# Row sums of the two widest diagonal pieces on GpSimd, and the running sum's matmuls at the block's end

## Chip, cores and metric

The kernel runs on one core of a Trainium2 chip. The metric is the device time of one execution in microseconds (us). Three executions of the kernel before took 2401.36, 2403.96 and 2404.28 us; the median, 2403.96 us, is the time before.

## What is computed

One decoder layer over 16 meta tokens and 2048 tokens of width 1024: a layer norm, one wide input projection, two token mixers side by side (attention with a forget gate, and a causal pooling), each gated, one output projection, and a last layer norm. The change touches the attention alone, 16 heads of 64 channels:

```python
s = jnp.einsum('bqhd,bkhd->bhqk', q_blk, k).astype(jnp.float32) * scale
s = s + jnp.transpose(c_blk, (0, 2, 1))[..., :, None] - c_k[:, :, None, :]
mask = key_pos[None, :] <= q_pos[:, None]
s = jnp.where(mask[None, None], s, -jnp.inf)
p = jax.nn.softmax(s, axis=-1).astype(v.dtype)
return jnp.einsum('bhqk,bkhd->bqhd', p, v)
```

The softmax needs the sum over all keys of the exponentials, for every query. That row sum is what the change moves about.

## The kernel before

**Stages.** Up to about 1350 us the kernel normalizes, projects and pools. Then comes the attention, until about 2225 us, with the output projection of the pooling half mixed into it; the rest of the output projection and the last layer norm follow.

**Blocks and units.** The attention works through 64 blocks, one for a head h and a group j of 512 queries (`seqn`, L763: j = 0 to 3 of one head after the other; the last two heads are interleaved). A block is a list of units (`units`, L903). A unit is one PSUM bank of up to 512 columns: 4j + 1 units with one tile of 128 keys against all 512 queries (the last of these, number 4j, lies on the diagonal and is masked in part), one unit 4j + 1 with the 400 queries from column 112 on, and a last unit 4j + 2 with three short pieces of 272, 144 and 16 columns. So a block has 4j + 3 units: 3, 7, 11 or 15.

**What a unit does.** `emit_s` (L959): two matmuls make the scores `s` in PSUM (four banks), a third adds the mask on the diagonal. ScalarE writes the exponential as `ph` in TensorE's rounded format, and once more in full precision over `s`. `emit_pl` (L996): VectorE subtracts `ph` from that, which is the rest `pl`; it also frees the bank of `s`. `emit_pv` (L1015), four units later (`LAG`): TensorE multiplies `ph` with the values into `xo`, and `pl` with the values, and with two columns of ones beside them, into `yo` (one PSUM bank). The ones give the row sum of `pl`.

**The row sum of `ph`.** It goes into the same `yo` and is made in two ways. For the units on the diagonal (4j, 4j + 1 and the three pieces) TensorE multiplies `ph` with `zo`, zeros and two columns of ones: `yo<-ph,zo`. For the units ahead of the diagonal, which only blocks with j of 1 or more have, GpSimd adds pairs of `ph` tiles: the first pair into `acc`, later ones into `tu` (three buffers). VectorE adds each `tu` to `acc` three units later. At unit 4j + 2, ahead of that unit's `pl`, VectorE adds the last `tu`, rounds `acc` to `th` and takes the rest `tl`; TensorE multiplies both with `zo` in the block's last `emit_pv`, ahead of the `pl` matmuls.

**Order.** `Ordered` (L78) chains the instructions of TensorE, VectorE, ScalarE and GpSimd, each in the order in which the code is written; only SyncE, which issues all DMAs, is ordered by the scheduler. The loop at L1085 takes one unit m a round: `emit_s(m)`, then some matmuls of the output projection (`fill`; about twice as many on units ahead of the last two as on those, none in the first 24 rounds), `emit_pl(m)`, `emit_pv(m - 4)`, loads for what comes, and every second round `service`. That one does what is due of the gating of finished blocks: GpSimd multiplies `araw` by two loaded tiles (`rb` and `sg`) and later makes `am`, VectorE makes the first half of `am`.

After a block's last `emit_pv`, ScalarE copies `yo` out (`c`), and VectorE adds it to `xo` (`t`, `araw`).

Of the kernel before, what the change touches and what calls it, by code (L numbers as in the profile page):

```python
# [40 lines left out]
def kernel(  # L41
# [917 lines left out]
    def emit_s(m):  # L959
# [28 lines left out]
        if i < 4 * j and i % 2:  # L988
            tag = "acc" if i == 1 else "tu"
            tu = bp.tile([P, 512], F32, tag=tag, name=tag, bufs=2 if i == 1 else 3)  # L990
            if i == 1:
                accs[n] = tu
            nc.gpsimd.tensor_tensor(out=tu, in0=f32(units_state[m - 1][0]), in1=f32(ph), op=ALU.add)
            units_tu[m] = tu

    def emit_pl(m):  # L996
        n, i, u, nu = seq[m]
        h, j = seqn[n]
        if 6 <= i and i % 2 == 0:
            nc.vector.tensor_tensor(out=accs[n], in0=accs[n], in1=units_tu.pop(m - 3), op=ALU.add)  # L1000
            if i == 4 * j + 2:
                th = bp.tile([P, 512], F32R, tag="th", name="th")
                tl = bp.tile([P, 512], F32R, tag="tl", name="tl")
                nc.vector.tensor_copy(out=th, in_=accs[n])
                nc.vector.tensor_tensor(out=tl, in0=accs[n], in1=f32(th), op=ALU.subtract)
                accs[n] = (th, tl)
        ps, ph, pl, off = late_pl.pop(m)
# [4 lines left out]
    late_pl = {}  # L1012
    xy = {}

    def emit_pv(m):  # L1015
# [9 lines left out]
        np_ = len(places)  # L1025
        full = i < 4 * j
        for idx, (kt, q0, w, off) in enumerate(places):
# [6 lines left out]
            )  # L1034
            if not full:
                mm(yo[0 : DH + 2, q0:512], zo, ph[:, sl], start=first, stop=False)
        if last_u and j:
            for t in accs.pop(n):
                mm(yo[0 : DH + 2, :], zo, t, start=False, stop=False)
        for idx, (kt, q0, w, off) in enumerate(places):  # L1040
            v = vc[:, j] if w == NM else vt[:, kt]
            mm(
                yo[0 : DH + 2, q0:512], v[:, DH:], pl[:, off : off + w],
                start=full and i == 0 and idx == 0, stop=last_u and idx == np_ - 1,
            )
        if last_u:
            c1 = bp.tile([65, 512], F32, tag="c1", name="c1", bufs=2)
# [37 lines left out]
    for m in range(nseq + LAG):  # L1085
# [11 lines left out]
        if m < nseq:  # L1097
            emit_pl(m)
        if m >= LAG:
            emit_pv(m - LAG)  # L1100
# [133 lines left out]
```

## Time and profile before

| | |
|---|---|
| median of three runs | 2403.96 us |
| the profiled execution | 2404.49 us, its span 2402.8 us |
| TensorE busy, share of the span | 2336.9 us, 97% |
| VectorE | 1427.3 us, 59% |
| ScalarE | 959.5 us, 40% |
| GpSimd | 719.3 us, 30% |
| granted TensorE clock, mean | 0.992 |

The profiled execution's own time is 1.7 us longer than the span from its first to its last instruction. In the profile PE is TensorE, DVE is VectorE, ACT is ScalarE, POOL is GpSimd, SP is SyncE. L86 is the helper through which every instruction is issued, so instructions are told apart by their tiles, out<-in.

### The profile page before, as it was taken

To read this page: it belongs to the slowest core of one execution; us is meant where nothing else is said; L and a number is where in the kernel's file an instruction comes from. 1 tells how busy PE (TensorE), PEld (TensorE's weight loads), DVE (VectorE), ACT (ScalarE), POOL (GpSimd) and SP (SyncE) were. 2 spreads that over 40 slices of the span, in tenths; PEclk is the share of its full clock that TensorE was granted. 3 is DMA by queue.
4 is the path that set the end of the run, shared out by engine and by line. 5 is a ranking of instruction groups with operands and counts; after the bars stand their busy time and mean duration, and the time that the engine had idled before them with its cause. 6 is when DMAs were issued, how large, how long until landed. Compare 5 with 4: busy or idle time off the path is not lost.

```text
span 2402.8 us, 32724 instructions
## 1 busy us (share of the span) xinstructions
PE 2336.9 (97%) x11706; PEld 1934.7 (81%) x11706; DVE 1427.3 (59%) x2116; ACT 959.5 (40%) x1813; POOL 719.3 (30%) x531
## 2 busy tenths in 40 slices
PE   6999999999999999999999999999999999999998
PEld 5778798898988989888887777777777777776787
DVE  6641145644655456545534288788788877777357
ACT  4430221212112211121111487777777777776000
POOL 4730021222313404140001135444353534444000
PEclk9999999999999999999999999999999999999999
DMA  7853231222212222222222666675665657555955
GB/s 246 268 164 97 58 95 61 89 63 83 88 61 89 78 67 89 61 90 78 77 68 89 165 190 195 177 210 165 199 183 178 204 168 221 168 170 160 294 184 166
DMA packets 317506, 333.59 MB, mean 139 GB/s; under 512 B 27744, under 2 KB 241072, under 8 KB 317312
## 3 DMA queue, kind: packets, MB, share of 16 engines
q1 hardware_dynamic: 317344, 331.51, 45.0%
q8 instruction: 92, 1.51, 0.3%
q14 instruction: 70, 0.57, 0.1%
HBM read 207.43 MB, written 124.00 MB: 138 GB/s over the span
## 4 chain that ended last, share of the span: by engine, by line
PE 91%; DVE 3%; DMA 2%; ACT 1%; issue 1%; POOL 0%; SPq 0%; DVEq 0%; ACTq 0%; POOLq 0%
PE d L86 60%; PE s L86 12%; PE yo L86 8%; PE mx L86 6%; PE xo L86 5%; DMA xm<-xa 1%; PE tr L86 1%; DVE pl L86 1%; ACT ph L86 0%; DMA wu<-in_wut_dram 0%; DMA xt<-in_x_dram 0%; DVE s L86 0%; DMA wv<-in_wv_dram 0%; ACT s L86 0%; DVE mxs L86 0%
## 5 line engine op out<-in xcount | busy, mean ns | idle before, releaser
L86 PE MATMUL d<-hh,wh 128*128 128x412 f32 (+2 forms) x1472 | 561.5, 381 | 0.0
L86 PE MATMUL d<-hl,wh 128*128 128x412 f32 (+2 forms) x1472 | 538.7, 366 | 0.0
L86 PE MATMUL d<-hh,wl 128*128 128x412 f32 (+2 forms) x1472 | 538.5, 366 | 0.0
L86 DVE TENSOR_REDUCE mxs<-mx 128x1 f32<-128x912 f32 (+14 forms) x416 | 358.0, 864 | 279.4 <-PE mx L86 274.8
L86 DVE TENSOR_TENSOR pl<-s,ph 128x512 fp32r<-128x512 f32 (+2 forms) x576 | 375.3, 663 | 179.0 <-ACT s L86 168.4
L86 ACT ACTIVATE ph<-s 128x512 fp32r<-128x512 f32 (+2 forms) x576 | 334.7, 581 | 178.3 <-PE s L86 167.2
L86 PE MATMUL d<-wh,xm 128*128 128x512 f32 x1024 | 354.8, 403 | 3.9 <-DMA xm<-xa 3.9
L86 ACT ACTIVATE s<-s 128x512 f32<-128x512 f32 (+2 forms) x576 | 332.9, 578 | 0.0
L86 PEld LDWEIGHTS d<-hl,wh 128*128 128x128 f32 x1472 | 278.5, 189 | 23.1
L86 PEld LDWEIGHTS d<-hh,wl 128*128 128x128 f32 x1472 | 277.2, 188 | 23.4
L86 PEld LDWEIGHTS d<-hh,wh 128*128 128x128 f32 x1472 | 280.8, 191 | 18.1
L86 PE MATMUL s<-qa,ka 68*128 68x512 f32 (+4 forms) x704 | 263.3, 375 | 15.4 <-DVE pl L86 13.6
L86 POOL TENSOR_TENSOR wl<-wst,wh 128x1024 fp32r<-128x1024 f32 x40 | 96.2, 2404 | 576.7 <-ACT wh L86 576.6
L86 PE MATMUL s<-qb,kb 128*128 128x512 f32 (+4 forms) x704 | 252.6, 360 | 0.0
L86 POOL TENSOR_TENSOR tu<-ph 128x512 f32<-128x512 f32 x144 | 192.8, 1341 | 135.4 <-ACT ph L86 118.7
L86 PE MATMUL xo<-ph,vt 128*128 128x512 f32 (+3 forms) x640 | 233.2, 368 | 0.0
L86 PEld LDWEIGHTS d<-wh,xm 128*128 128x128 f32 x1024 | 193.5, 190 | 43.5 <-issue 2.4
L86 PE MATMUL yo<-pl,vt 128*66 128x512 f32 (+3 forms) x640 | 223.3, 365 | 1.8 <-ACT c L86 1.8
L86 PE MATMUL mx<-ka,qa 66*128 66x512 f32 (+5 forms) x704 | 199.4, 350 | 6.6 <-ACT qa L86 3.8
L86 PE MATMUL d<-wl,xm 128*128 128x512 f32 x512 | 205.6, 402 | 0.0
L86 PEld LDWEIGHTS s<-qa,ka 68*128 68x128 f32 x704 | 134.9, 192 | 69.0 <-DVE pl L86 26.3
L86 PEld LDWEIGHTS mx<-ka,qa 66*128 66x128 f32 x704 | 133.0, 190 | 23.8 <-ACT qa L86 5.2
(143 smaller groups left out, 3069.3 us busy)
## 6 DMA issues: line engine op xcount, KB each, us to landing
xm<-xp SPq DMA_DIRECT2D x32, 1024.0 KB
xm<-xa SPq DMA_DIRECT2D x20, 1024.0 KB
vd<-vs SPq DMA_DIRECT2D x32, 512.0 KB
vt<-vd SPq DMA_DIRECT2D x64, 256.0 KB
qb<-kqd SPq DMA_DIRECT2D x64, 256.0 KB
xa<-am SPq DMA_DIRECT2D x32, 512.0 KB
xp<-pm SPq DMA_DIRECT2D x32, 412.0 KB
kqd<-lo SPq DMA_DIRECT2D x64, 206.0 KB
```

Of the source, the lines that this page charges most:

```text
L86: return in_order(f(*a, **k))
```

## The change

For blocks with j of 1 or more, the `ph` of units 4j and 4j + 1 no longer goes through `zo` on TensorE. GpSimd adds it to the block's last `tu` (all 512 columns, then the 400 from column 112 on). Only the three short pieces, and the blocks with j = 0, keep `yo<-ph,zo`. The last `acc` addition with `th` and `tl` moves from unit 4j + 2, ahead of its `pl`, to the round after, behind the `pl` of the next block's first unit (`emit_sums`, called between `emit_pl` and `emit_pv`). In the block's last `emit_pv` the two matmuls with `th` and `tl` come last, and the `pl` matmuls ahead of them; `yo` is started by the first `pl` matmul.

```diff
--- before.py
+++ after.py
@@ -992,18 +992,19 @@
                 accs[n] = tu
             nc.gpsimd.tensor_tensor(out=tu, in0=f32(units_state[m - 1][0]), in1=f32(ph), op=ALU.add)
             units_tu[m] = tu
+        if j and 4 * j <= i < nu - 1:
+            tu = units_tu[m - 1 - (i - 4 * j)]
+            nc.gpsimd.tensor_tensor(
+                out=tu[:, u[0][1] :], in0=tu[:, u[0][1] :], in1=f32(ph[:, :off]), op=ALU.add
+            )
 
     def emit_pl(m):
         n, i, u, nu = seq[m]
         h, j = seqn[n]
-        if 6 <= i and i % 2 == 0:
+        if 6 <= i <= 4 * j and i % 2 == 0:
             nc.vector.tensor_tensor(out=accs[n], in0=accs[n], in1=units_tu.pop(m - 3), op=ALU.add)
-            if i == 4 * j + 2:
-                th = bp.tile([P, 512], F32R, tag="th", name="th")
-                tl = bp.tile([P, 512], F32R, tag="tl", name="tl")
-                nc.vector.tensor_copy(out=th, in_=accs[n])
-                nc.vector.tensor_tensor(out=tl, in0=accs[n], in1=f32(th), op=ALU.subtract)
-                accs[n] = (th, tl)
+        if j and i == 4 * j + 2:
+            sums_due.append((m + 1, n))
         ps, ph, pl, off = late_pl.pop(m)
         nc.vector.tensor_tensor(
             out=pl[:, :off], in0=ps[:, :off], in1=f32(ph[:, :off]), op=ALU.subtract
@@ -1011,6 +1012,20 @@
 
     late_pl = {}
     xy = {}
+    sums_due = deque()
+
+    def emit_sums(m):
+
+        while sums_due and sums_due[0][0] <= m:
+            at, n = sums_due.popleft()
+            nc.vector.tensor_tensor(
+                out=accs[n], in0=accs[n], in1=units_tu.pop(at - 4), op=ALU.add
+            )
+            th = bp.tile([P, 512], F32R, tag="th", name="th")
+            tl = bp.tile([P, 512], F32R, tag="tl", name="tl")
+            nc.vector.tensor_copy(out=th, in_=accs[n])
+            nc.vector.tensor_tensor(out=tl, in0=accs[n], in1=f32(th), op=ALU.subtract)
+            accs[n] = (th, tl)
 
     def emit_pv(m):
         n, i, u, nu = seq[m]
@@ -1023,7 +1038,6 @@
         xo, yo = xy[0], xy[1]
         last_u = i == nu - 1
         np_ = len(places)
-        full = i < 4 * j
         for idx, (kt, q0, w, off) in enumerate(places):
             first = i == 0 and idx == 0
             sl = slice(off, off + w)
@@ -1032,17 +1046,18 @@
                 xo[:, q0:512], v[:, 0:P], ph[:, sl],
                 start=first, stop=last_u and idx == np_ - 1,
             )
-            if not full:
+            if last_u or not j:
                 mm(yo[0 : DH + 2, q0:512], zo, ph[:, sl], start=first, stop=False)
-        if last_u and j:
-            for t in accs.pop(n):
-                mm(yo[0 : DH + 2, :], zo, t, start=False, stop=False)
         for idx, (kt, q0, w, off) in enumerate(places):
             v = vc[:, j] if w == NM else vt[:, kt]
             mm(
                 yo[0 : DH + 2, q0:512], v[:, DH:], pl[:, off : off + w],
-                start=full and i == 0 and idx == 0, stop=last_u and idx == np_ - 1,
-            )
+                start=bool(j) and i == 0 and idx == 0, stop=last_u and idx == np_ - 1 and not j,
+            )
+        if last_u and j:
+            th, tl = accs.pop(n)
+            mm(yo[0 : DH + 2, :], zo, th, start=False, stop=False)
+            mm(yo[0 : DH + 2, :], zo, tl, start=False, stop=True)
         if last_u:
             c1 = bp.tile([65, 512], F32, tag="c1", name="c1", bufs=2)
             nc.scalar.copy(out=c1, in_=yo[0:65, :])
@@ -1096,6 +1111,7 @@
             fill(k)
         if m < nseq:
             emit_pl(m)
+        emit_sums(m)
         if m >= LAG:
             emit_pv(m - LAG)
         if 0 < m < nseq:
```

VectorE at the end of the j = 2 block of an odd head (the next block is j = 3 of the same head; `pl` 128x400 and 128x432 are the block's last two units, the `pl` of 512 columns behind them is the next block's first, the reciprocal belongs to the gating):

```order
 L86 TENSOR_TENSOR pl<-s,ph 128x400
-L86 TENSOR_TENSOR acc<-acc,tu 128x512
-L86 CAST th<-acc 128x512
-L86 TENSOR_TENSOR tl<-acc,th 128x512
-L86 TENSOR_TENSOR pl<-s,ph 128x432
-L86 TENSOR_TENSOR pl<-s,ph 128x512
+L86 TENSOR_TENSOR pl<-s,ph 128x432
+L86 TENSOR_TENSOR pl<-s,ph 128x512
+L86 TENSOR_TENSOR acc<-acc,tu 128x512
+L86 CAST th<-acc 128x512
+L86 TENSOR_TENSOR tl<-acc,th 128x512
 L86 RECIPROCAL st<-st 128x8
```

The three sum instructions stand two `pl` later than before.

GpSimd at the same place, before (three `tu` of the block, then the next block's `acc`, then the gating):

```order
L86 TENSOR_TENSOR tu<-ph 128x512 x3
L86 TENSOR_TENSOR acc<-ph 128x512
L86 TENSOR_TENSOR araw<-araw,rb 128x512
L86 TENSOR_TENSOR araw<-araw,sg 128x512
L86 TENSOR_TENSOR tu<-ph 128x512 x2
```

and of the changed kernel:

```order
L86 TENSOR_TENSOR tu<-ph 128x512 x3
L86 TENSOR_TENSOR tu<-tu,ph 128x512
L86 TENSOR_TENSOR tu<-tu,ph 128x400
L86 TENSOR_TENSOR acc<-ph 128x512
L86 TENSOR_TENSOR araw<-araw,rb 128x512
L86 TENSOR_TENSOR araw<-araw,sg 128x512
L86 TENSOR_TENSOR tu<-ph 128x512 x2
```

Two additions into the last `tu` stand between it and the next block's `acc<-ph`.

TensorE at the end of that block (the last `emit_pv`, from its first piece to the next scores), before:

```order
L86 MATMUL xo<-ph,vt 128x272
L86 MATMUL yo<-ph,zo 66x272
L86 MATMUL xo<-ph,vt 128x144
L86 MATMUL yo<-ph,zo 66x144
L86 MATMUL xo<-ph,vc 128x16
L86 MATMUL yo<-ph,zo 66x16
L86 MATMUL yo<-th,zo 66x512
L86 MATMUL yo<-tl,zo 66x512
L86 MATMUL yo<-pl,vt 66x272
L86 MATMUL yo<-pl,vt 66x144
L86 MATMUL yo<-pl,vc 66x16
L86 MATMUL s<-qa,ka 128x512
```

and of the changed kernel:

```order
L86 MATMUL xo<-ph,vt 128x272
L86 MATMUL yo<-ph,zo 66x272
L86 MATMUL xo<-ph,vt 128x144
L86 MATMUL yo<-ph,zo 66x144
L86 MATMUL xo<-ph,vc 128x16
L86 MATMUL yo<-ph,zo 66x16
L86 MATMUL yo<-pl,vt 66x272
L86 MATMUL yo<-pl,vt 66x144
L86 MATMUL yo<-pl,vc 66x16
L86 MATMUL yo<-th,zo 66x512
L86 MATMUL yo<-tl,zo 66x512
L86 MATMUL s<-qa,ka 128x512
```

The matmuls with `th` and `tl` stand directly ahead of the next scores. In the two units before this one, `yo<-ph,zo` of 512 and of 400 columns is gone; over the whole program TensorE's order has 11674 rows in place of 11770, GpSimd's 537 in place of 441, and ScalarE's is the same.

## Rows read from the trace of the kernel before

**Rows 1.** The page, busy time of TensorE in the whole span: us, share of the span, instructions.

```profile
PE 2336.9 (97%) x11706; PEld 1934.7 (81%) x11706; DVE 1427.3 (59%) x2116; ACT 959.5 (40%) x1813; POOL 719.3 (30%) x531
```

**Rows 2.** The windows view: three stretches of the attention, busy us of each engine in each.

```profile
core 0: us, PE busy (x) PEld busy (x) DVE busy (x) ACT busy (x) POOL busy (x), PEclk, DMA share, GB/s
1352.00:1400.00 48.00, 42.68 (x213) 30.89 (x212) 33.73 (x53) 37.56 (x74) 15.58 (x13) 1.00 0.77 211
1400.00:2175.00 775.00, 769.07 (x3995) 593.19 (x3993) 615.38 (x956) 583.33 (x1113) 343.44 (x260) 1.00 0.62 183
2175.00:2225.00 50.00, 43.13 (x208) 32.08 (x207) 39.53 (x57) 30.89 (x61) 21.78 (x15) 0.97 0.62 182
```

**Rows 3.** The waits view from 1400 to 2175 us: engine and tile that waited, for whom, us in total, times, the longest.

```profile
ACT ph L86 <- PE s L86: 158.9, 344, 1.7
DVE pl L86 <- ACT s L86: 117.2, 197, 1.6
...
DVE acc L86 <- POOL tu L86: 8.1, 7, 1.3
...
PE s L86 <- DVE pl L86: 5.9, 10, 0.9
```

**Rows 4.** The timeline of TensorE: start, length in us, instruction. The `yo<-ph,zo` matmuls of 512 and 400 columns of one block, each with the matmul behind it.

```profile
1597.15 0.40 PE L86 MATMUL yo<-ph,zo 128*66 128x512 f32 x1
1597.38 0.39 PE L86 MATMUL yo<-pl,vt 128*66 128x512 f32 x1
...
1598.72 0.34 PE L86 MATMUL yo<-ph,zo 128*66 128x400 f32 x1
1598.89 0.35 PE L86 MATMUL yo<-pl,vt 128*66 128x400 f32 x1
```

**Rows 5.** The lines view from 1352 to 2225 us for GpSimd's additions (count | busy us, mean ns | idle before), and the tile view of the same stretch for the three sum instructions of VectorE (ns: shortest/median/longest).

```profile
L86 POOL TENSOR_TENSOR tu<-ph 128x512 f32<-128x512 f32 x144 | 192.8, 1341 | 135.4 <-ACT ph L86 118.7 <-DVE pl L86 16.2
...
L86 DVE TENSOR_TENSOR acc<-acc,tu x144: 640/786/1783, 1373.3 to 2209.3; 128x512 f32<-128x512 f32 x144
...
L86 DVE CAST th<-acc x48: 426/427/1410, 1374.0 to 2210.6; 128x512 fp32r<-128x512 f32 x48
L86 DVE TENSOR_TENSOR tl<-acc,th x48: 691/693/1666, 1374.5 to 2212.0; 128x512 fp32r<-128x512 f32 x48
```

**Rows 6.** The timelines of VectorE and of GpSimd at two places where both work at once, near 2194 us and near 1385 us.

```profile
2193.66 0.68 DVE L86 TENSOR_TENSOR acc<-acc,tu 128x512 f32<-128x512 f32 x1
2194.37 1.38 DVE L86 CAST th<-acc 128x512 fp32r<-128x512 f32 x1
2195.79 1.63 DVE L86 TENSOR_TENSOR tl<-acc,th 128x512 fp32r<-128x512 f32 x1
...
2193.82 1.65 POOL L86 TENSOR_TENSOR am<-araw,am 128x512 fp32r<-128x512 f32 x1 [0.97 <-DVE am L86]
2195.43 1.44 POOL L86 TENSOR_TENSOR acc<-ph 128x512 f32<-128x512 f32 x1
...
1384.80 0.67 DVE L86 TENSOR_TENSOR acc<-acc,tu 128x512 f32<-128x512 f32 x1
...
1384.57 2.05 POOL L86 TENSOR_TENSOR tu<-ph 128x512 f32<-128x512 f32 x1 [0.36 <-ACT ph L86]
```

**Rows 7.** The timelines of ScalarE, VectorE, GpSimd and TensorE at the end of the j = 2 block of an odd head, near 1650 us; in brackets the idle time before the instruction and what ended it.

```profile
1646.95 0.60 ACT L86 ACTIVATE s<-s 128x512 f32<-128x512 f32 x1
...
1645.02 0.68 DVE L86 TENSOR_TENSOR acc<-acc,tu 128x512 f32<-128x512 f32 x1
...
1646.19 0.69 DVE L86 TENSOR_TENSOR tl<-acc,th 128x512 fp32r<-128x512 f32 x1
...
1647.58 0.69 DVE L86 TENSOR_TENSOR pl<-s,ph 128x512 fp32r<-128x512 f32 x1 [0.18 <-ACT s L86]
...
1648.29 1.29 POOL L86 TENSOR_TENSOR acc<-ph 128x512 f32<-128x512 f32 x1 [5.38 <-ACT ph L86]
1649.55 1.30 POOL L86 TENSOR_TENSOR araw<-araw,rb 128x512 f32<-128x512 f32 x1
...
1651.70 0.39 PE L86 MATMUL yo<-tl,zo 128*66 128x512 f32 x1
...
1652.14 0.48 PE L86 MATMUL s<-qa,ka 68*128 68x512 f32 x1
```

**Rows 8.** The timelines of VectorE, GpSimd and TensorE at the end of the j = 3 block of an odd head, near 1670 us, and TensorE's row at the same place in three other pairs of heads.

```profile
1668.67 1.58 DVE L86 TENSOR_TENSOR acc<-acc,tu 128x512 f32<-128x512 f32 x1
...
1670.75 0.69 DVE L86 TENSOR_TENSOR tl<-acc,th 128x512 fp32r<-128x512 f32 x1
1671.36 1.20 DVE L86 TENSOR_TENSOR pl<-s,ph 128x432 fp32r<-128x432 f32 x2
...
1668.41 1.29 POOL L86 TENSOR_TENSOR am<-araw,am 128x512 fp32r<-128x512 f32 x1 [1.70 <-DVE am L86]
...
1672.01 0.50 PE L86 MATMUL s<-qa,ka 68*128 68x512 f32 x1 [0.91 <-DVE pl L86]
...
1464.57 0.50 PE L86 MATMUL s<-qa,ka 68*128 68x512 f32 x1 [0.67 <-DVE pl L86]
...
1568.38 0.50 PE L86 MATMUL s<-qa,ka 68*128 68x512 f32 x1 [0.67 <-DVE pl L86]
...
1776.42 0.50 PE L86 MATMUL s<-qa,ka 68*128 68x512 f32 x1 [0.90 <-DVE pl L86]
```

## Prediction

> **What bounds the kernel now.** I read the windows first, since the change touches only the attention stage. From 1400 to 2175 us TensorE is busy 769 of 775 us at granted clock 1.00, while VectorE has 615, ScalarE 583 and GpSimd 343 [rows 2]; over the whole span TensorE has 97% [rows 1]. Busy time alone does not prove that TensorE sets the pace, because the matmuls in a trace overlap: one of 512 columns is shown 0.40 us long, but the next starts 0.23 us later [rows 4]. So I read the waits next. In the stretch TensorE waits 5.9 us in all, ten times, each time for VectorE's `pl`, which frees the PSUM bank that the next `s` wants; the other way ScalarE waits 159 us for `s` from TensorE and VectorE 117 us for ScalarE [rows 3]. The chain TensorE, ScalarE, VectorE therefore stands behind TensorE, and a matmul taken out there is time taken off the end. At the two edges this does not hold: in 1352 to 1400 TensorE is busy 42.7 of 48 us, in 2175 to 2225 43.1 of 50 [rows 2].
>
> **What goes.** 48 blocks (16 heads, j = 1 to 3) lose two `yo<-ph,zo` matmuls each, one of 512 and one of 400 columns: 96 of 11706. Start to start they take 1597.38 - 1597.15 = 0.23 us and 1598.89 - 1598.72 = 0.17 to 0.18 us [rows 4], 0.41 us a block, 19.7 us for all 48. Two of these blocks end before 1400 and three after 2175, where TensorE idles anyway; I give those five back (2 us) and count 43 x 0.41 = **-17.6 us**.
>
> The Trainium skill (TensorE: Matmul & The Clock Gate, "Back-to-back issue gap") says that in a stream of weight loads and matmuls 512 columns cost about 131 ns sustained, and that the isolated gap of some 216 ns overstates it. By that figure, and an estimate of 0.11 us for 400 columns worked out from it and the 81 ns that the page has for 128, this term would be about 10 us and the forecast some 7 us later. The trace disagrees (0.23 us), in a stream that is full.
>
> **What is added to GpSimd.** 48 adds of 512 and 48 of 400 columns. The add of 512 takes 1.34 us there [rows 5]; 400 columns, in proportion, about 1.05. That is 48 x 2.4 = 115 us, which brings GpSimd from 343 to about 450 of 775 us in the stretch. No one waits for this work except the last `acc` of the block, and that was moved too. Two adds behind each other take 2.4 us; `acc` now comes two units later than before, which is about 3 us: the `yo<-ph,zo` of two units in a row start at 1597.15 and 1598.72 [rows 4]. So the wait is hidden unless GpSimd is held up: VectorE waited for it 8.1 us, seven times, in the stretch, and TensorE did not feel all of that [rows 3]. What stands behind GpSimd in turn, the gating of `araw` and `am` and the DMAs that SyncE issues after them, comes later by up to 2.4 us; the attention output that they store is read only late, and I cost it at nothing.
>
> **What is moved on VectorE.** `acc`, `th` and `tl` (three instructions, same number as before) leave the place ahead of the block's last `pl` and go behind the first `pl` of the next block. This has a good side and a bad side.
>
> The good side: that last `pl`, 432 wide, no longer stands behind 1.9 us of sums. At 1668.67 `acc`, `th` and `tl` ran until 1671.44, the `pl` behind them began at 1671.36, and TensorE's next `s` stood still for 0.91 us until it was done [rows 8]. This is the end of the j = 3 block of an odd head; the rows at 1464.57, 1568.38 and 1776.42 are the same place in other pairs of heads (0.67, 0.67 and 0.90 us). With the sums behind it `pl` goes at once. But there `acc` must then wait for GpSimd (`am` ran until 1669.70, and the second new add stands behind it), and `tl` arrives about when it is wanted, so I take **-2 us** of the 5.9, with bounds 0 and -5.9.
>
> The bad side is slack. I work out one place, the block ending near 1650 [rows 7]. Before, `tl` ended at 1646.88 and TensorE took it at 1651.70: 4.8 us to spare. After, the `pl` of the next block's first unit still starts at 1647.58, because ScalarE gave it its input only at 1647.55; it ends at 1648.27 and `acc` follows. TensorE wants `tl` just before the next `s`: 1652.14, less 0.41 for the matmuls gone, less 0.23 for `tl` itself, 1651.50. Undisturbed the three take 1645.02 to 1646.88, 1.86 us, so they end at 1650.13 and nothing waits. But at 1648.29 GpSimd starts the next block's `acc<-ph`, with `araw` right behind it. What such a meeting costs is seen at 2193.66 [rows 6]: `acc` started 0.16 us ahead of GpSimd's `am` and took its usual 0.68, the `am` took 1.65; `th` then stood until `am` was over (1.38 us in place of 0.43), and `tl` until GpSimd's next one was (1.63 in place of 0.69): 3.76 us from start to end. By that `tl` ends at 1648.27 + 3.76 = 1652.03, and TensorE waits **0.53 us**. If GpSimd comes first in all three meetings, each takes its maximum, 1.78, 1.41 and 1.67 us [rows 5], 4.9 with the gaps, and the wait is 1.7 us.
>
> Meetings of this kind are due where the next block also has j of 1 or more, since only these start with an `acc<-ph`: two ends per head, 28 in the stretch. Bounds for the mean wait at each: 0 (they miss each other) and 1.7 (GpSimd first everywhere). I take half of 0.53, because `tl` runs free wherever GpSimd has nothing queued behind `acc<-ph`: 28 x 0.27 = **+7.5 us**.
>
> A new wait of a microsecond or less should not touch the clock: the 0.91 us stand at 1672 lies in a stretch that was granted 1.00 [rows 2, 8].
>
> Last, `yo` ends with `th` and `tl` in place of the short `pl` matmuls; same matmuls, same sum, no change. The PSUM bank is released at the same point of TensorE's order.
>
> **Sum.** -17.6 + 7.5 - 2 = -12.1 us. The profiled execution took 2404.49 us, 0.5 above the median of the three runs, so 2392.4 there and 2392 as a median.
>
> **Rivals.**
> Full gain. The sums and GpSimd miss each other, or `tl` is always in time, all 5.9 us of waits go, and the edges keep their 2 us: -19.7 - 5.9 = -25.6, 2378. For it: undisturbed there are 1.4 us to spare at the place worked out. Against it: `acc<-ph` starts within 0.02 us of the moment at which `acc` becomes free to start, and the order, not chance, sets that.
>
> No gain. TensorE's matmuls go, but ScalarE's and VectorE's work becomes the pace, and the time stays at 2399 to 2409. For it: the edges, where this is the case now. Against it: 117 and 159 us of waits on the other side [rows 3], far more than 17.6.
>
> Slower. GpSimd comes first at the block ends, and the waits for `tl` are 1.7 us at all 28: 47.6 - 17.6 = +30, about 2434. It decides itself at a mean wait of 17.6 / 28 = 0.63 us per such end: above it the change loses. For it: the starts are so near each other that 0.1 us turns the order, and GpSimd has some 100 us more to do in the stretch, so that it more often still has the port. Against it: at 1384.57 GpSimd started 0.23 us ahead and VectorE's `acc` still took its usual 0.67, with GpSimd at 2.05 [rows 6], so VectorE wins a near tie.
> The Trainium skill (SBUF — State Buffer, "Who interferes with whom") speaks against the change here: a VectorE instruction with two SBUF inputs, or a copy in a two-port mode, and a GpSimd instruction that reads SBUF exclude each other, and whoever issues first holds the port for the whole instruction. The long `th` and `tl` agree with it. By its "first" GpSimd would win at 1384.57, and the time would lean to this rival; the row there says otherwise.
>
> That the change does not do what it says I rule out: the order of TensorE has 96 rows fewer, that of GpSimd 96 more.
>
> **How the numbers follow.** A measurement of this kernel can tell about 0.2%, 4.8 us, from no change. Forecast (2386 to 2399): 0.53. Full gain (below 2386): 0.20. No gain (2399 to 2409): 0.15. Slower (above 2409): 0.12. So faster 0.73, same 0.15, slower 0.12. The range runs from the full gain, 2379, to the mid of the no-gain case, 2403, which leaves out about 0.12 + 0.07.
>
> **What would show it.** TensorE has 96 matmuls fewer and `yo<-ph,zo` of 512 and 400 columns 16 times each; GpSimd has 96 `tu<-tu,ph`. If the steps are right, the long stretch is some 12 us shorter with VectorE and ScalarE at the same busy time; a new row "TensorE `yo` waits for VectorE `th` or `tl`" stands at 5 to 15 us; the wait of `s` for `pl` is below 5.9; the medians of `th` and `tl` rise above the 427 and 693 ns that they have now [rows 5]. The slack step is wrong if TensorE never waits for `tl`, or if it waits more than 18 us. The first step is wrong if TensorE's waits stay small and the time does not fall. The GpSimd step is wrong if VectorE's wait of `acc` for `tu` grows far beyond 8.1 us.

## The result, and the profile after

| | before | changed |
|---|---|---|
| median of 6 runs each, same chip | 2402.28 us | 2414.50 us |
| lowest to highest | 2400.57 to 2404.28 | 2411.67 to 2417.40 |
| span of the profiled execution | 2402.8 us | 2411.9 us |
| granted TensorE clock, mean | 0.992 | 0.987 |

The ratio is 1.005, 95% interval 1.004 to 1.006: the change costs 12 us. The forecast was 2392, with 2403 as its upper end; the time is above the range, and the sign is wrong.

The page of the changed kernel, answering [rows 1]:

```profile
PE 2332.4 (97%) x11610; PEld 1928.4 (80%) x11610; DVE 1467.4 (61%) x2116; ACT 957.9 (40%) x1813; POOL 852.1 (35%) x627
```

Its windows view, answering [rows 2] (the last stretch ends at 2235 here, since the attention ends later):

```profile
1352.00:1400.00 48.00, 40.76 (x191) 29.59 (x190) 34.90 (x48) 35.66 (x70) 18.47 (x16) 0.93 0.71 199
1400.00:2175.00 775.00, 755.28 (x3875) 580.43 (x3874) 644.46 (x953) 578.25 (x1108) 460.15 (x345) 0.99 0.62 184
2175.00:2235.00 60.00, 51.90 (x239) 38.19 (x237) 47.01 (x66) 35.94 (x70) 33.80 (x25) 0.91 0.51 152
```

TensorE has its 96 matmuls fewer, GpSimd its 96 additions more. But in the long stretch TensorE now idles 20 of 775 us where it idled 6, VectorE is busy 29 us longer with no more instructions, and the granted clock is below that of before in every stretch. The waits view says on whom TensorE waits. From 1400 to 2175 us, as in [rows 3]:

```profile
DVE acc L86 <- POOL tu L86: 13.7, 14, 1.2
PE yo L86 <- DVE tl L86: 12.3, 19, 1.4
...
PE s L86 <- DVE pl L86: 5.1, 9, 1.0
...
PE yo L86 <- DVE th L86: 1.9, 2, 1.6
```

And with both edges, 1352 to 2235 us:

```profile
PE yo L86 <- DVE tl L86: 14.4, 23, 1.4
PE s L86 <- DVE pl L86: 9.8, 14, 2.1
PE yo L86 <- DVE th L86: 6.1, 5, 2.1
```

The wait of `s` for `pl` is hardly smaller (5.1 for 5.9 us), and a new one has come: 14.2 us for `th` and `tl` in the stretch, 20.5 with the two edges. The tile view shows why, answering [rows 5] (ns: shortest/median/longest):

```profile
L86 POOL TENSOR_TENSOR acc<-ph x48: 1277/1420/1749, 1365.5 to 2207.1; 128x512 f32<-128x512 f32 x48
L86 DVE CAST th<-acc x48: 426/1396/1499, 1375.8 to 2224.4; 128x512 fp32r<-128x512 f32 x48
L86 DVE TENSOR_TENSOR tl<-acc,th x48: 691/693/1781, 1376.2 to 2224.8; 128x512 fp32r<-128x512 f32 x48
```

The median `th` took 427 ns before and takes 1396 now: at most block ends it stands until GpSimd is done. The median of `tl` stays at 693; its longest is 1781. One of the worst places, the j = 1 end of head 5, in the timelines of VectorE, GpSimd and TensorE:

```profile
1635.04 0.69 DVE L86 TENSOR_TENSOR pl<-s,ph 128x512 fp32r<-128x512 f32 x1
1635.64 0.68 DVE L86 TENSOR_TENSOR acc<-acc,tu 128x512 f32<-128x512 f32 x1
1636.36 1.40 DVE L86 CAST th<-acc 128x512 fp32r<-128x512 f32 x1
1637.79 1.78 DVE L86 TENSOR_TENSOR tl<-acc,th 128x512 fp32r<-128x512 f32 x1
...
1635.74 1.73 POOL L86 TENSOR_TENSOR acc<-ph 128x512 f32<-128x512 f32 x1 [2.76 <-ACT ph L86]
1637.75 1.27 POOL L86 TENSOR_TENSOR tu<-ph 128x512 f32<-128x512 f32 x1 [0.28 <-ACT ph L86]
...
1637.81 0.44 PE L86 MATMUL yo<-th,zo 128*66 128x512 f32 x1
1639.62 0.45 PE L86 MATMUL yo<-tl,zo 128*66 128x512 f32 x1 [1.37 <-DVE tl L86]
```

`acc` starts 0.10 us ahead of GpSimd's `acc<-ph` and takes its usual 0.68, while GpSimd takes 1.73. Then `th` stands until GpSimd is through (1.40). By then the next pair's `ph` is there, `tu<-ph` starts 0.04 us ahead of `tl`, and `tl` stands too (1.78). From `acc` to `tl` the chain takes 3.93 us in place of 1.86, and TensorE stands still for 1.37 us.

### The profile page after: what moved, and what is told of

Its sections match the earlier page's. It is cut to its first block, busy times and chain, and to the rows that moved or that the text cites. A ratio compares the mean times of both kernels' runs of the same rounds, so it can differ in the third digit from the quotient of the medians.

```text
span 2411.9 us, 32689 instructions
## 1 busy us (share of the span) xinstructions
PE 2332.4 (97%) x11610; PEld 1928.4 (80%) x11610; DVE 1467.4 (61%) x2116; ACT 957.9 (40%) x1813; POOL 852.1 (35%) x627
## 3 DMA queue, kind: packets, MB, share of 16 engines
q8 instruction: 91, 1.49, 0.3%
## 4 chain that ended last, share of the span: by engine, by line
PE 83%; DVE 7%; DMA 3%; issue 2%; ACT 2%; POOL 2%; SPq 1%; ACTq 0%; DVEq 0%; POOLq 0%
PE d L86 57%; PE s L86 9%; PE mx L86 6%; PE yo L86 5%; PE xo L86 4%; DVE acc L86 1%; POOL tu L86 1%; DVE th L86 1%; DVE pl L86 1%; SPq L86 1%; DVE tl L86 1%; ACT ph L86 1%; ACT s L86 1%; PE tr L86 1%; POOL am L86 0%
## 5 line engine op out<-in xcount | busy, mean ns | idle before, releaser
L86 DVE TENSOR_TENSOR pl<-s,ph 128x512 fp32r<-128x512 f32 (+2 forms) x576 | 369.4, 660 | 159.2 <-ACT s L86 148.0
L86 PEld LDWEIGHTS s<-qb,kb 128*128 128x128 f32 x704 | 136.8, 194 | 21.7
```

The lines of the kernel that those rows point to most:

```text
L86: return in_order(f(*a, **k))
```

## The experiments

All are timed against the kernel before on the same chip, in the same series; its median was 2402.26 to 2403.15 us. The table has for each kernel the median, the ratio with its interval, the span of the profiled execution as a difference from 2402.8, TensorE's waits in `s` and `yo` (the sum of these rows of the waits view from 1352 to 2235 us; 16.8 before; the waits of `d`, the output projection's matmuls, are left out: 3.0 before, none in the changed kernel, at most 5.3), the mean granted clock, and a sum made from these, explained below. Spans, waits and clocks are of the one profiled execution, which lies up to 4.2 us from the median: e1's is the fastest of its runs, e14's the slowest.

| kernel | median us | ratio | span | waits | clock | sum |
|---|---|---|---|---|---|---|
| changed | 2414.50 | 1.0050 (1.0040 to 1.0060) | +9.1 | 33.0 | 0.987 | +8.6 |
| e1 matmuls removed only | 2393.18 | 0.9957 (0.9943 to 0.9972) | -15.5 | 18.0 | 0.989 | -11.5 |
| e2 sums moved only | 2410.53 | 1.0034 (1.0023 to 1.0045) | +3.4 | 23.1 | 0.993 | +3.9 |
| e3 additions only | 2427.23 | 1.0099 (1.0084 to 1.0114) | +24.3 | 28.8 | 0.987 | +24.3 |
| e4 sums one `pl` earlier | 2395.90 | 0.9973 (0.9961 to 0.9985) | -9.5 | 19.9 | 0.989 | -9.5 |
| e5 `acc<-ph` issued later | 2413.64 | 1.0044 (1.0032 to 1.0057) | +10.6 | 32.6 | 0.988 | +5.8 |
| e6 matmuls twice | 2419.35 | 1.0065 (1.0052 to 1.0078) | +15.5 | 11.8 | 0.990 | +19.7 |
| e7 e4, late at odd j = 3 ends | 2393.28 | 0.9960 (0.9947 to 0.9972) | -11.9 | 21.5 | 0.991 | -12.7 |
| e8 e4 and e5 | 2399.98 | 0.9987 (0.9978 to 0.9996) | -7.4 | 18.8 | 0.987 | -5.8 |
| e9 moved and removed | 2398.56 | 0.9982 (0.9973 to 0.9991) | -7.4 | 24.9 | 0.990 | -6.9 |
| e10 moved and added | 2416.66 | 1.0060 (1.0047 to 1.0073) | +14.8 | 23.7 | 0.989 | +14.3 |
| e11 `acc<-ph` behind `tu<-ph` | **2384.48** | 0.9923 (0.9910 to 0.9937) | -20.0 | 14.3 | 0.990 | -17.6 |
| e12 e7, edges as before | 2389.05 | 0.9943 (0.9930 to 0.9955) | -15.5 | 17.0 | 0.992 | -15.9 |
| e13 e11's order in the kernel before | 2401.19 | 0.9993 (0.9984 to 1.0002) | -4.1 | 15.6 | 0.993 | -3.6 |
| e14 e4 with e11's order | 2388.50 | 0.9934 (0.9922 to 0.9946) | -14.9 | 17.3 | 0.991 | -16.9 |

The **sum** has three terms: the matmuls (19.7 us for 96, 16.0 for the 78 of e12), the difference of the waits, and the difference of what the lower clock takes, span x (1 - mean clock), since work at half clock takes nearly twice its time (in the changed kernel matmuls of 512 columns start 0.43 us apart at 1641.42, at half clock, and 0.24 at 1644.28, at full clock). For the changed kernel: -19.7 + (33.0 - 16.8) + (2411.9 x 0.013 - 2402.8 x 0.008) = -19.7 + 16.2 + 12.1 = +8.6, where the span grew by 9.1. The clock is given to 0.001, so the last term is good to some 2 us: added up from the stretches at half clock in the two traces, it is 10.4 in place of 12.1. The matmul term is -19.7 where they are gone (-16.0 in e12), +19.7 in e6 and 0 elsewhere. The sum misses the span by at most 0.8 us in nine kernels and by 1.6 to 4.8 in the other six, to both sides. With a clock term this coarse, the closest of these matches are luck. But the three terms hold most of the differences, and the experiments can be read term by term.

### The three parts of the change, alone and in pairs

**e1**, the matmuls go, all else as before:

```diff
-            if not full:
+            if last_u or not j:
                 mm(yo[0 : DH + 2, q0:512], zo, ph[:, sl], start=first, stop=False)
```

> The kernel before without the 96 matmuls yo<-ph,zo of 512 and 400 columns; nothing takes their place, so the row sums of these two units are left out. It prices the removal alone. If TensorE sets the pace in the attention and only the late sums spoil the change, 18 to 20 us below the kernel before, about 2384, with TensorE's waits as before. If ScalarE and VectorE are the pace already, within 5 us of the kernel before.

It brought 9 us (median), between the two expectations, and 15.5 in the profiled execution, the fastest of its runs. By the table the larger part of what is missing is clock: its term is 7.0 us, that of the waits 1.2. Part went into old waits that grew. At the two places where TensorE stood 0.67 us for `pl` at the end of an odd head's j = 3 block [rows 8] it now stands 1.07 and 1.08. The first of them, in its timeline:

```profile
1461.88 0.50 PE L86 MATMUL s<-qa,ka 68*128 68x512 f32 x1 [1.07 <-DVE pl L86]
```

TensorE comes 0.41 us earlier and waits 0.40 us longer: at an end that VectorE sets, a removed matmul is worth nothing.

**e2**, the changed kernel without the additions and with its matmuls back:

```diff
-        if j and 4 * j <= i < nu - 1:
-            tu = units_tu[m - 1 - (i - 4 * j)]
...
-            if last_u or not j:
+            if i >= 4 * j:
```

> The changed kernel without the additions on GpSimd and with the 96 matmuls back on TensorE: only acc, th and tl later on VectorE and last on TensorE. If the late chain acc, th, tl, which meets GpSimd's acc<-ph of the next block, is the cause, TensorE waits for tl here too, 10 to 15 us in all (0.41 us less at each place, since TensorE comes there later), and the kernel is 8 to 18 us above the kernel before. If the additions on GpSimd are the cause (they hold the port and slow VectorE everywhere), within 4 us of the kernel before.

The move alone costs 8 us. TensorE waits 9.6 us for `th` and `tl`, and the median of `th` is already 1396 ns. The profiled execution is one of the fastest of its runs, with the highest clock (0.993; the others have 0.988 to 0.992), so the trace holds only 3.4 of these 8 us.

**e3**, the kernel before with 96 additions of the same shapes, at the same places, into a tile that no one reads:

```diff
             units_tu[m] = tu
+        if j and 4 * j <= i < nu - 1:
+            nc.gpsimd.tensor_tensor(
+                out=scr[:, u[0][1] :], in0=scr[:, u[0][1] :], in1=f32(ph[:, :off]), op=ALU.add
+            )
```

> The kernel before plus 96 additions on GpSimd of the same size and at the same places as the change's, into a scratch tile that nobody reads; everything else as before. If the late chain is the cause, 0 to 6 us above the kernel before, with VectorE some 20 us busier. If the additions themselves are the cause, 20 us or more above it.

This is the miss of the first series: work for which no one waits costs 25 us. VectorE, GpSimd and TensorE at the j = 3 end of head 5:

```profile
1678.37 1.57 DVE L86 TENSOR_TENSOR acc<-acc,tu 128x512 f32<-128x512 f32 x1
1679.97 1.14 DVE L86 CAST th<-acc 128x512 fp32r<-128x512 f32 x1
1681.15 0.69 DVE L86 TENSOR_TENSOR tl<-acc,th 128x512 fp32r<-128x512 f32 x1
...
1678.10 1.29 POOL L86 TENSOR_TENSOR am<-araw,am 128x512 fp32r<-128x512 f32 x1 [0.43 <-DVE am L86]
1679.35 1.48 POOL L86 TENSOR_TENSOR scr<-scr,ph 128x400 f32<-128x400 f32 x1
...
1682.41 0.62 PE L86 MATMUL s<-qa,ka 68*128 68x512 f32 x1 [2.06 <-DVE pl L86]
```

The windows view of the stretch behind it:

```profile
1682.00:1690.00 8.00, 7.59 (x32) 6.04 (x33) 4.92 (x9) 3.84 (x7) 2.28 (x2) 0.79 0.74 199
```

Behind `am`, where GpSimd had nothing to do before, it now has an addition, and `th`, 0.43 us by its median [rows 5], takes 1.14. The `pl` queued behind it comes later, and TensorE's wait, 0.91 us at the same end [rows 8], becomes 2.06; in the 8 us behind it the clock is granted at 0.79. Of the 24.3 us of span, 12.0 are such waits and some 12 the clock (10.7 when the stretches at half clock are added up).

**e9** and **e10** are the other pairs: the changed kernel without the additions, and with the matmuls put back.

```diff
-        if j and 4 * j <= i < nu - 1:
-            tu = units_tu[m - 1 - (i - 4 * j)]
```

> The changed kernel without GpSimd's 96 additions: the sums late, the matmuls gone, so the row sums of the two widest diagonal pieces are left out. The sums' move alone (additions and matmuls both as before) left TensorE 9.6 us of waits for th and tl, the whole change 20.7. If the additions make the other 11 us, by keeping GpSimd on the port, the waits are near 10 us here and the time falls to 2396 to 2402. If TensorE makes them itself, since without the matmuls it comes to th 0.41 us earlier at each block end, the waits stay near 20 us and the time at 2410 to 2414.

```diff
-            if last_u or not j:
+            if i >= 4 * j:
```

> The changed kernel with the 96 matmuls put back beside the additions (the row sums of the two units count double). If the additions make the waits, they are still near 20 us and the time rises by what the matmuls cost when they were issued twice, 17 us: about 2431. If the waits come from TensorE's being 0.41 us early at each end, they fall to about 10 us here, and the time rises by only 5 to 8 us, to 2419 to 2422.

The waits view of e9, 1352 to 2235 us:

```profile
PE yo L86 <- DVE tl L86: 11.0, 18, 1.2
...
PE yo L86 <- DVE th L86: 3.4, 4, 1.0
```

and of e10:

```profile
PE yo L86 <- DVE tl L86: 6.8, 7, 1.4
PE yo L86 <- DVE th L86: 3.3, 3, 2.0
```

In e10 the waits came as the second theory had it, the time below both. Neither theory has it alone. With the sums moved, the waits for `th` and `tl` are 9.6 us; 14.4 with the matmuls gone too, 10.1 with the additions too, 20.5 with both. Each part adds to the waits mostly when the other is there. TensorE's row at each end says where: at the 26 ends of j = 1 and j = 2 blocks of heads 1 to 13 the waits are 3.7 us in e2 and in e10, 9.3 in e9, and 10.4 in the changed kernel. There the removal adds most, since TensorE comes earlier; the additions add most of theirs at the ends of j = 3 blocks and at the edges. In times (of series whose kernel before differed by 0.9 us at most), the removal was worth 9.1 us in the kernel before, 12.0 on top of the move (2410.53 to 2398.56), and 2.2 on top of move and additions (2416.66 to 2414.50).

**e6** asked whether a matmul costs what its start-to-start time says:

```diff
             if not full:
                 mm(yo[0 : DH + 2, q0:512], zo, ph[:, sl], start=first, stop=False)
+            if j and 4 * j <= i < nu - 1:
+                mm(yo[0 : DH + 2, q0:512], zo, ph[:, sl], start=False, stop=False)
```

> The kernel before with the 96 matmuls that the change removes issued twice (the row sums of these two units count double, so the output is not the reference's). If TensorE sets the pace at 0.23 and 0.17 us each, this adds 19.7 us, less a few at the edges: 2418 to 2422. If such a matmul costs less in the stream than its start-to-start time says, the addition is as small as the 9 us that their removal gave: 2411. If it is +18 or more, then the removal's missing part was lost to waits that came up when TensorE ran earlier, not to the price of a matmul.

Issued twice they add 16.8 us (2402.56 to 2419.35). In the profiled execution TensorE's old waits shrink under them by 5.0 us, and the clock's term grows by as much. So the two about cancel, and the 96 matmuls cost 15.5 us (span) to 16.8 us (median): most of the 19.7 us of the start-to-start times. What the removal alone failed to bring went to the clock and to waits. The 131 ns of the Trainium skill (TensorE: Matmul & The Clock Gate, "Back-to-back issue gap") gave an estimate of some 10 us; this run speaks against that figure here.

### Curing the meeting

**e4** takes the sums one `pl` earlier, behind the last `pl` of their own block:

```diff
-            sums_due.append((m + 1, n))
+            sums_due.append((m, n))
...
-                out=accs[n], in0=accs[n], in1=units_tu.pop(at - 4), op=ALU.add
+                out=accs[n], in0=accs[n], in1=units_tu.pop(at - 3), op=ALU.add
```

> The changed kernel with acc, th and tl one pl earlier, behind the block's last pl and ahead of the next block's first. If the late chain is the cause, TensorE's waits for th and tl fall from 20 us to under 5, and the time to 2384 to 2392; at the ends of the j = 3 blocks of odd heads VectorE waits longer for GpSimd, with up to 1 us at each of seven places for TensorE. If the additions are the cause, it stays at 2408 or above.

It gives 2395.90, between the two expectations: the median of `th` is back at 427 ns, and the waits at the ends of j = 1 blocks are gone but for 0.59 us at the last; in all, 6.5 us of waits for `th` and `tl` are left. **e7** keeps the late place behind an odd head's j = 3 block (`m + (j == 3 and h % 2)`), where VectorE in e4 waits 1.4 us for GpSimd's last addition:

> The early-sums kernel, but behind the j = 3 block of an odd head the sums stand where the changed kernel has them (one pl later), since there VectorE waits 1.4 us for GpSimd's last addition with a pl queued behind it. If that wait is hidden, as TensorE's rows say (0.15 us for pl and 0.25 for th at each of these ends), the time is that of the early sums within 2 us, 2394 to 2397. If it costs what VectorE's row says, the time falls by 4 to 8 us, to 2388 to 2392.

It gives 2393.28, 2.6 us less than e4, in another series and with overlapping intervals of the ratio: not told apart.

**e5** meant to take GpSimd's first addition of the next block out of the way, by issuing it with the second pair:

```diff
+            if i == 3:
+                nc.gpsimd.tensor_tensor(
+                    out=accs[n], in0=f32(units_state[m - 3][0]), in1=f32(units_state[m - 2][0]), op=ALU.add
+                )
+            if i > 1:
+                nc.gpsimd.tensor_tensor(out=tu, in0=f32(units_state[m - 1][0]), in1=f32(ph), op=ALU.add)
+                units_tu[m] = tu
```

> The changed kernel with one GpSimd addition put later: the next block's first acc<-ph is issued with its second pair (unit 3) instead of at unit 1. Nothing else moves. If the waits for th and tl come from meeting this addition, th is back at 0.43 us at the ends of j = 1 blocks, the waits there (10.9 of 20.7 us in the changed kernel) are gone, and the time falls by 10 to 14 us, more than the waits themselves if the half-clock stretches go with them: 2400 to 2404. If the meeting partner is any GpSimd work, whichever comes next, the waits only change places and the time stays within 3 us of the changed kernel. If the chain is late by itself, whatever GpSimd does, it also stays.

The time stayed. At the ends of j = 1 blocks the edit did not do what it was written for. GpSimd at that of head 5 in e5:

```profile
1637.82 1.73 POOL L86 TENSOR_TENSOR acc<-ph 128x512 f32<-128x512 f32 x1 [2.76 <-ACT ph L86]
```

The whole run is 2.08 us later here, and everything else is as it was: idle 2.76 us, start when its `ph` is there, 1.73 long. Nothing else stood ahead of it in GpSimd's queue, so issuing it later moved nothing, and the waits at the 13 ends of this kind are 8.1 us, as in the changed kernel. At the ends of j = 2 and j = 3 blocks of odd heads the edit did change the order: the gating's two products now run ahead of `acc<-ph`, where they ran behind it. GpSimd and TensorE at the j = 2 end of head 5 in e5:

```profile
1652.45 1.29 POOL L86 TENSOR_TENSOR araw<-araw,rb 128x512 f32<-128x512 f32 x1 [0.77 <-DMA rb<-rd]
1653.82 1.29 POOL L86 TENSOR_TENSOR araw<-araw,sg 128x512 f32<-128x512 f32 x1
1655.08 1.74 POOL L86 TENSOR_TENSOR acc<-ph 128x512 f32<-128x512 f32 x1
...
1658.84 0.44 PE L86 MATMUL yo<-tl,zo 128*66 128x512 f32 x1 [1.19 <-DVE tl L86]
```

VectorE's `acc` starts at 1654.14 beside a product and takes 1.53 us, `th` then 1.40 and `tl` 1.65; TensorE waits 1.19 us, where it waits 0.37 in the changed kernel. At the 13 ends of j = 2 blocks the waits rise from 2.3 to 4.1 us. So here the partner is whatever GpSimd does next, not `acc<-ph` alone. **e8** put the same edit into e4:

> Early sums and the late first pair together. If the meeting of the sums with acc<-ph is the whole trouble, early sums have already cured it and this adds nothing: 2394 to 2397. If other meetings of acc<-ph count (with pl, th at the ends of even j = 2 blocks, 1.40 us), 2 to 4 us less. If the late pair pushes acc<-ph and tu<-ph together so that VectorE's first acc+tu waits for GpSimd, it is slower than the early sums by 2 to 5 us.

At 2399.98 it is 4 us above e4, though the intervals of the two ratios overlap. Its waits are no larger (18.8 us); what differs in the profiled execution is the clock, 0.987, and what lowered it is open. `acc<-ph` changes places with the gating's products here as in e5; the waits for `th` and `tl` at the ends of j = 1 and j = 2 blocks of heads 1 to 13 are none in e4 and none here.

**e11** makes the start wait for data: `acc<-ph` is issued behind the `tu<-ph` of unit 3, so it can't begin before that unit's `ph` is there.

```diff
+            if i > 1:
+                nc.gpsimd.tensor_tensor(out=tu, in0=f32(units_state[m - 1][0]), in1=f32(ph), op=ALU.add)
+                units_tu[m] = tu
+            if i == 3:
+                nc.gpsimd.tensor_tensor(
+                    out=accs[n], in0=f32(units_state[m - 3][0]), in1=f32(units_state[m - 2][0]), op=ALU.add
+                )
```

> The changed kernel with GpSimd's acc<-ph issued behind the tu<-ph of unit 3, so that it cannot start until that unit's ph is there (issuing it later with nothing ahead of it had not moved its start at all). Then GpSimd has nothing of the next block to do while acc, th and tl run at the ends of j = 1 blocks. If the meeting there makes the waits, the 10.9 us at these ends shrink below 3 and the time falls by 8 to 14 us, to 2400 to 2406. If tl is late there without any meeting, the waits stay above 8 us and the time within 3 us of the changed kernel.

2384.48: 18.7 us below the kernel before, and far below the range expected. The 30 us to the changed kernel come from the order of GpSimd's work alone, an engine that is busy 35% of the span (at the ends of j = 2 and j = 3 blocks of odd heads the gating's products pass ahead of `acc<-ph` too, as in e5). The j = 1 end of head 5 again, VectorE, GpSimd and TensorE:

```profile
1625.22 0.68 DVE L86 TENSOR_TENSOR acc<-acc,tu 128x512 f32<-128x512 f32 x1
1625.93 0.43 DVE L86 CAST th<-acc 128x512 fp32r<-128x512 f32 x1
1626.39 0.69 DVE L86 TENSOR_TENSOR tl<-acc,th 128x512 fp32r<-128x512 f32 x1
...
1627.32 1.30 POOL L86 TENSOR_TENSOR tu<-ph 128x512 f32<-128x512 f32 x1 [4.17 <-ACT ph L86]
1628.58 1.29 POOL L86 TENSOR_TENSOR acc<-ph 128x512 f32<-128x512 f32 x1
...
1627.17 0.42 PE L86 MATMUL yo<-th,zo 128*66 128x512 f32 x1
1627.43 0.40 PE L86 MATMUL yo<-tl,zo 128*66 128x512 f32 x1
```

The tile view of e11:

```profile
L86 DVE CAST th<-acc x48: 426/427/1416, 1375.4 to 2195.6; 128x512 fp32r<-128x512 f32 x48
```

Its waits view, 1352 to 2235 us:

```profile
PE s L86 <- DVE pl L86: 6.7, 9, 1.7
...
PE yo L86 <- DVE tl L86: 3.1, 8, 1.2
PE yo L86 <- DVE th L86: 2.5, 2, 2.1
```

The chain takes 1.86 us, ends at 1627.08 and is wanted at 1627.43: no wait, with 0.35 us to spare. TensorE's waits for `th` and `tl` fall from 20.5 to 5.6 us (3.3 of it at one place near the end), its other waits from 12.5 to 8.7, and the clock rises to 0.990. These are 18.7 us of waits and 7.5 of clock, 26.2 of the 29.1 us between the two spans. **e13** gives the same order to the kernel before, where nothing late hangs on it:

> The kernel before with the first pair's acc<-ph behind the tu<-ph of unit 3, and nothing else: how much of the 18.7 us that this order and the change gave together belongs to the order alone. In the kernel before, the sums stand ahead of the block's last pl and meet am and araw rather than acc<-ph, and TensorE has almost no waits there to win. If the order only cures what the change brings on, the time stays within 3 us of the kernel before, 2400 to 2405. If acc<-ph slows pl and acc everywhere, it falls by 5 to 10 us by itself.

2401.19, not to be told from no change. The 18.7 us therefore belong mostly to the change, once its meeting is gone: against e13 it brings 2401.19 - 2384.48 = 16.7 us. **e14** has early sums and this order:

> Early sums together with acc<-ph behind the tu<-ph of unit 3 (in the early-sums kernel with a late pair it had stood ahead of that tu<-ph). If late tl and the meeting with acc<-ph are one and the same trouble, either cure is enough and both give what the better one gives, 2384 +- 3. If the early place has a trouble of its own, the 1.4 us for which VectorE waits at the ends of the j = 3 blocks of odd heads with pl queued behind, it stays above the late place with the same order: 2388 to 2396.

2388.50: with the meeting cured the early place brings nothing more than the late one, rather less (4 us, with overlapping intervals of the ratios). Its waits of `s` for `pl` (10.0 us, e11 6.7) and VectorE's for GpSimd's `tu` (19.3, e11 14.3) fit the trouble that was named, a `pl` queued behind the waiting `acc`.

**e12** takes e7 and leaves nine blocks at the two edges as they were:

```diff
+    def moved(n):
+        h, j = seqn[n]
+        return j and (h, j) not in EDGE
...
-            if last_u or not j:
+            if last_u or i >= 4 * j and not moved(n):
```

> The fastest kernel so far (early sums, late only behind the j = 3 blocks of odd heads, 2393.3 us) with nine blocks at the two edges, (0,1), (0,2), (13,3) and all of heads 14 and 15, done as in the kernel before: matmuls, no additions, sums ahead of the last pl. There TensorE waits 7.2 us for th and tl in the early-sums kernels, and the removed matmuls (9 x 0.41 = 3.7 us) bring little because TensorE idles anyway. If these waits are the additions' doing, 2 to 4 us less: 2389 to 2391. If the edges are bound by VectorE whatever is done, the same time within 1.5 us; if the matmuls count there as elsewhere, up to 4 us more.

2389.05, 4 us below e7 in another series (the intervals of the ratios overlap a little, 0.9930 to 0.9955 and 0.9947 to 0.9972), though it gives up 3.7 us of removed matmuls; TensorE's waits are 17.0 us in place of 21.5. At the nine blocks it leaves out the removal, the additions and the move together, so which of the three matters there is not shown.

## Why the prediction was wrong

**What bounds the kernel** was right: TensorE sets the pace in the long stretch. e6 shows it (+16.8 for matmuls whose start-to-start times add up to 19.7 us), and the three-term sum rests on it.

**What goes, -17.6.** The price holds in the main (e6), but not as a saving on its own: 9.1 us in the kernel before, 2.2 in the one that was changed; in e11's order the whole change brings 16.7. Wherever TensorE then stands before something of VectorE's, being 0.41 us early is 0.41 us more wait. The prediction gave this back at five edge blocks only.

**The slack step, +7.5, is the step that failed**, by what was left out of it, not by its mechanism. The mechanism is as written: `acc` comes first and runs free, `th` and `tl` stand. At the very place that was worked out, the j = 2 end of head 5, the rows of the changed kernel are

```profile
1653.71 0.68 DVE L86 TENSOR_TENSOR acc<-acc,tu 128x512 f32<-128x512 f32 x1
1654.43 1.40 DVE L86 CAST th<-acc 128x512 fp32r<-128x512 f32 x1
1655.86 1.67 DVE L86 TENSOR_TENSOR tl<-acc,th 128x512 fp32r<-128x512 f32 x1
...
1657.59 0.45 PE L86 MATMUL yo<-tl,zo 128*66 128x512 f32 x1 [0.37 <-DVE tl L86]
```

0.68, 1.40 and 1.67 us where 0.68, 1.38 and 1.63 were taken, and a wait of 0.37 for the 0.53 worked out. But that was one place of many, and a lenient one. A j = 1 end has less slack, and the trace of before showed it at head 5 (VectorE, then TensorE):

```profile
1631.38 0.69 DVE L86 TENSOR_TENSOR tl<-acc,th 128x512 fp32r<-128x512 f32 x1
...
1635.50 0.39 PE L86 MATMUL yo<-tl,zo 128*66 128x512 f32 x1
```

`tl` is 3.43 us ahead of its use there, against 4.82 at the place worked out [rows 7]: 1.39 us less, so the same working gives 0.53 + 1.39 = 1.9 us of wait, and 1.37 came. Added up over TensorE's row at each end, the 28 ends of this kind in the stretch cost 13.4 us: the 13 of j = 1 in heads 1 to 13 cost 8.1 (1.15 to 1.49 at six of them, next to nothing at the others), the 13 of j = 2 cost 2.3, and the j = 3 ends of heads 13 and 14, which another j = 3 block follows, cost 3.1. That is 0.48 each for the 0.27 taken. The halving ("`tl` runs free wherever GpSimd has nothing queued behind `acc<-ph`") failed as well: at j = 1 ends `tu<-ph` of the next pair met `tl` as its `ph` arrived, without being queued. And the 20 other ends, which were costed at nothing because no `acc<-ph` follows or because they lie at the edges, took another 7 us, 6.3 of it at the edges: 20.5 in all against 7.5. The prediction's own sign, a row of 5 to 15 us in the long stretch, was met with 14.2; it was set at up to twice the term, and left the edges out.

**The clock at nothing** failed, and cost most of the rest: 12.1 us by the mean clock, 10.4 when the stretches at half clock are added up, 5.1 of it in the long stretch and 5.7 at the two edges, with 0.4 less outside them. Windows of the changed kernel, each just behind a wait for `tl` at a j = 1 end (1.37, 1.36, 1.22 us):

```profile
1640.00:1645.00 5.00, 5.00 (x17) 3.72 (x16) 4.31 (x9) 2.73 (x5) 1.29 (x1) 0.66 0.31 85
...
1747.00:1752.00 5.00, 5.00 (x24) 3.84 (x23) 4.90 (x10) 4.25 (x8) 1.29 (x1) 1.00 0.23 66
...
1801.00:1806.00 5.00, 5.00 (x16) 3.74 (x15) 4.15 (x7) 2.84 (x6) 1.29 (x1) 0.66 0.64 197
```

Full clock is 1.00, 2.4 GHz; 0.66 means that 3.4 of these 5 us were granted at half, 1.2 GHz. "A microsecond or less" was inferred from one wait of 0.91 us, and the waits that came were longer. Behind these three, alike in length, it fell twice and once not, and it stayed at 1.00 behind the three other waits of 1.15 to 1.23 us at j = 1 ends (1587.90, 1694.96 and 1961.42). So the length of a wait alone doesn't tell.

**GpSimd's additions at nothing** failed. From e9 to the changed kernel they cost 16 us (2398.56 to 2414.50): 6.1 us of waits for `th` and `tl`, 7.4 of clock by the sum's term, the rest not assigned. They were counted as work that no one waits for; but they lengthen sums that someone does wait for. Of the 6.1 us only 1.1 fall on the 26 ends of j = 1 and j = 2 blocks, 2.3 on the edges, 0.8 on the j = 3 ends of odd heads, and 1.9 on the j = 3 end of head 13: there VectorE stands 0.82 us for GpSimd's last addition, and its `acc` at 2103.78 then takes 1.76 us beside the next `acc<-ph`. In e11, with the same additions, the change brings 16.7 us, so little of that price is left, and it is not one of the additions as such. VectorE's own wait for `tu` grew from 8.1 to 13.7 us in the stretch, which was the sign named in the prediction, and TensorE felt little of it (0.25 us at each of three j = 3 ends, and these 1.9).

**The move's good side, -2**, was 0.8 in the long stretch: 5.9 to 5.1 us; with both edges the wait of `s` for `pl` fell from 13.6 to 9.8.

**The rivals.** The slower one had the right mechanism, with 1.7 us at all 28 ends; 0.48 came. It was put down with a break-even of 0.63 us per end, as though only these ends and no clock counted; with the clock and the other ends, 0.48 was enough to lose. The rule of the Trainium skill that was held against the change (SBUF — State Buffer, "Who interferes with whom": who issues first holds the shared port for the whole instruction) described this kernel better than it was given credit for. At 1635.64 `acc` was first by 0.10 us and ran free, at 1637.75 GpSimd was first by 0.04 and `tl` stood. The row at 1384.57 [rows 6] says otherwise, and from this one row the prediction took it that VectorE wins a near tie.

## What to carry to other kernels

Before moving a chain of instructions closer to its use, read its slack at every kind of place where it occurs, not at one, and add what it takes when another engine works beside it; the smallest slack decides, and it was in the trace of before. An engine that is 30% busy is no free place for work if its instructions lengthen those of a chain that is waited for: ask what runs beside the chain, not only who waits for the added work. If a meeting costs, order the other engine so that its start waits for data that comes later; issuing it later in a queue that is empty does nothing, and where other work is queued between, the chain meets that work in its place.

## What the runs showed of the hardware that was not expected

- Two engines that meet again and again take turns, so a chain of three VectorE instructions with 1.80 us of work took 3.93 us against GpSimd instructions that alone take 1.29 us each, and 4.65 where GpSimd was first all three times (e5, 1654.14 to 1658.79). In the changed kernel VectorE's held instructions end 0.29 and 0.55 us after GpSimd's (`th` at 1637.76 after 1637.47, `tl` at 1639.57 after 1639.02), so a `th` of 0.43 us becomes 1.40 next to one.
- GpSimd work without any reader, 132 us more of it busy (719.3 to 851.2), lengthened the kernel by 25 us (e3), about half through waits and half through the granted clock.
- The granted clock fell behind short waits, 1.2 to 2.1 us, and not behind each: 10 to 12 us of the changed kernel's time more than before is clock. What decides which of them does it stays open here.
